# Second feed-forward block: seven products from chunk 2 on, its first plain down inside the first pair, and another order in the mixer

## The chip, the cores and the metric

The kernel runs on one core of a Trainium2 chip. Its engines work side by side, each through its own list of instructions: PE (TensorE, matmuls into eight PSUM banks of 128 x 512 fp32), DVE (VectorE), ACT (ScalarE), POOL (GpSimd) and SP (SyncE, which here only issues loads). Instructions of different engines wait for each other by semaphores. The metric is the time of one execution on the device in microseconds (us), the median of several runs.

## The reference

One layer on x of 512 tokens by 1024, all in fp32: half a SwiGLU feed-forward block, a token mixer, half a second feed-forward block, each with an RMS norm before and after.

```python
def swiglu(x, w_gu, w_down):                     # w_gu 1024 x 5632, w_down 2816 x 1024
    gate, up = jnp.split(x @ w_gu, 2, axis=-1)
    return (jax.nn.silu(gate) * up) @ w_down

def hybrid_mixer(h, ...):
    proj = h @ w_in                              # x_lru 512, gate_lru 512, q 512, k 128, v 128
    ...
    y_lru = rg_lru(x_lru, ...) * jax.nn.gelu(gate_lru)     # convolution of width 4, gates, a linear scan over tokens
    y_attn = sliding_window_sink_attention(q, k, v, sinks) # window 128, blocks of 128 queries, 8 heads of 64
    y = jnp.concatenate([rms_norm(y_lru, g_lru_out), rms_norm(y_attn, g_attn_out)], axis=-1)
    return y @ w_o

def reference(x, ...):
    x = x + 0.5 * rms_norm(swiglu(rms_norm(x, ffn1_pre_g), ffn1_w_gu, ffn1_w_down), ffn1_post_g)
    x = x + rms_norm(hybrid_mixer(rms_norm(x, mix_pre_g), ...), mix_post_g)
    x = x + 0.5 * rms_norm(swiglu(rms_norm(x, ffn2_pre_g), ffn2_w_gu, ffn2_w_down), ffn2_post_g)
    return x
```

## The kernel before

**Numbers.** Each fp32 operand is split into two parts of the faster matmul format: a high part (a cast by ACT) and a low part (operand less high part, by DVE). A product is three matmuls: high x high, high x low, low x high. Names carry it: `whi`/`wlo` are the parts of a weight, `xh`/`xl` of the input, `hh`/`hl` of the hidden activations. Activations are kept turned: the width lies on the partitions, the 512 tokens along the row.

**Stages.** Block 1 (letter a), mixer (letters mx, q, gt, wo), block 2 (letter b). The 2816 hidden columns are 22 chunks of 128. In a block the first chunks are *plain* (`Hidden.classic`): gate and up of each chunk are 24 matmuls over 512 columns each. The rest comes in pairs of chunks (`Hidden.quad`): gate and up of two chunks are a 2 x 2 block product, which is made with seven half-size products instead of eight (Winograd's form). Each of the seven is 24 matmuls of 256 columns into one of three banks A, D, B; their weight operands are sums of blocks of the weight (units p, q, r, s, t, u, v of `add_quad`), their input operands are parts and sums of the input: b11, b21, b22 are parts of xh and xl themselves, t1 to t4 come from `Turned.sums` (four DVE sums of 128x256 and two ACT casts per slice k of four) and `Turned.lows` (the DVE low parts). The down product is plain for the first group (`first_down`: for each half dh of the width, four token blocks, a bank each, which ACT copies to a `stage` and POOL sends to memory), and of the seven-product kind for groups of four chunks (`seven_down`: 84 matmuls of 512 columns, partial results added in memory by POOL's transfers). In block 2 `CLASSIC2` = 6 chunks are plain, `GROUPS2` starts (0, 6), (6, 10), and three groups have a seven down.

**Weights.** `W` holds one list of raw loads and one list of units in the order in which PE takes them. `load` issues the next raw on SP's queue into one of five buffers of 1 MB (`NRAW`); a buffer comes free when its last unit is split. `round` (or `cast`) does ACT's cast of the next unit, `fill` DVE's low part. `take(ahead)` hands PE the next unit and first fills `ahead` units beyond it; `later(n, fn)` runs fn at the n-th take from now. In `add_quad` a sum of weight blocks is made in place in the raw buffer by DVE (`combine`), ahead of the cast that reads it. The rows of x for the residual (`x_rows`) occupy two of the five raw buffers from late in block 1 to the end of the mixer.

**Order.** It is written out by hand: each engine runs its instructions in the order in which the program issues them. The mixer interleaves, by hand, PE's gate products (`gt`, `pump`), scores, softmax (`exps`, `normalise`), transposes of the probabilities (`turn_p`, ACT copies `pa`, POOL's masked copies `pc`), values (`po`), the LRU (`decay_b`: DVE's `th`; `root`; `scan`) and gelu (`gelu_b`: DVE, then a tanh on ACT; `gelu_c`, `gelu_d`), and at the end the product with w_o (`wo`), whose weights are `whi_wo60`, `wlo_wo60` and so on.

**The mixer's end.** `boundary` makes the four token blocks' rows (`Rows.steps`: norm, residual, norm), transposes them (`turn`, `turned`) and runs the gate/up of chunks 0 and 1 of block 2 meanwhile, in halves of the tokens (`one`, then `k_high` and `k_low`, the products named `mn`). Then the rows are stored to `x_hbm` for the last residual, `classic` runs chunks 2 to 5 with the sums of k = 0, 1 between them, `Turned.blocks` makes the b11 copies (eight ACT casts), and `first_down` runs with the sums of k = 2, 3.

Of the kernel before, what the change touches and what calls it, by code (L numbers as in the profile page):

```python
# [8 lines left out]
F32 = mybir.dt.float32  # L9
# [24 lines left out]
CLASSIC1, CLASSIC2 = 4, 6  # L34
SEVEN_DOWN1, SEVEN_DOWN2 = (4, 16), (6, 18)
# [12 lines left out]
class Weights:  # L48
# [60 lines left out]
    def take(self, ahead=AHEAD):  # L109
        self.fill(1 + ahead, ahead >= AHEAD)  # L110
# [11 lines left out]
def tile_layer(ctx: ExitStack, tc: tile.TileContext, out: bass.AP, **ins: bass.AP):  # L122
# [72 lines left out]
    def add_quad(w_gu, f, name):  # L195
# [11 lines left out]
        def unit(block, n, pre=None):  # L207
            def cast(raw):
                assert ry < W.loaded
# [4 lines left out]
            def low(raw, hi, lo):  # L214
                dve.tensor_sub(lo, of(block), hi.bitcast(F32))

            W.unit(block[0], cast, low, pre)
# [58 lines left out]
    def add_layer(w_gu, wd, name, groups, classic, seven, done):  # L276

        for f0, f1 in groups:
            for f in range(max(f0, done), f1, 2):
                (add_gate_up if f < classic else add_quad)(w_gu, f, name)  # L280
# [250 lines left out]
    class Turned:  # L531


        def __init__(self, name, pre, forms=False):
            self.name, self.pre, self.t = name, pre, {}
# [16 lines left out]
        def sums(self, k):  # L552
# [12 lines left out]
            self.made = n, highs, (t13, t24)  # L565

        def lows(self, k):

            n, highs, xs = self.made
            for s, h, x, names in zip(("t13", "t24"), highs, xs, (("t1", "t3"), ("t2", "t4"))):  # L570
                lo = t2k(f"{s}l_{n}", F32R)
                dve.tensor_sub(lo, x, h.bitcast(F32))
                for i, m in enumerate(names):
                    self.t[m, k] = h[:, HALF[i]], lo[:, HALF[i]]

        def blocks(self):

            l, r = HALF
            for k in range(4):
                b11 = t2k(f"b11_{self.name}{k}", F32R)  # L580
                for x, sl in zip(self.xs[k], HALF):
                    act.copy(b11[:, sl], x.bitcast(F32)[:, l])
                self.t["b11", k] = b11[:, l], b11[:, r]
                for m, sl in (("b21", l), ("b22", r)):
                    self.t[m, k] = tuple(x[:, sl] for x in self.xs[k + 4])

    class Rows:


        def __init__(self, name, x, gain, scale, eps, nxt):  # L590
            self.name, self.x, self.scale, self.eps, self.nxt = name, x, scale, eps, nxt
# [32 lines left out]
        def steps(self, tb):  # L624
# [3 lines left out]
            for dh in range(2):  # L628
                x = self.x[tb][:, HALF_D[dh]]
                dve.scalar_tensor_tensor(x, self.z.pop((tb, dh)), self.rs, x, op0=ALU.mult, op1=ALU.add)  # L630
                self.sum_square(tb, dh, x, "x")
            yield
# [21 lines left out]
    def boundary(rows, produce, parts, turns, fills, ahead, name):  # L654
# [68 lines left out]
        W.fill(2)  # L723
        k_high(ws, banks, xs, r, range(KD))
# [1014 lines left out]
```

## Time and profile before

| | us |
|---|---|
| runs (3) | 858.18, 858.59, 859.12; median 858.59 |
| profiled execution | 858.53, span 856.3, granted clock 0.998 |
| PE busy | 845.0 (99%), 5534 matmuls |
| DVE busy | 656.8 (77%) |
| ACT busy | 529.2 (62%) |
| POOL busy | 153.6 (18%) |

A row of the timeline gives start, duration, engine, line, operation, output <- inputs, shapes, how many follow each other, and in square brackets how long the engine sat idle before it and what ended that. Starts on PE are the more exact ends of a stage: a matmul's own duration overlaps the next one. On the chain of waits a row is start, length and what ran. "A, x3" means three such instructions in a row. The span of the profile is 2.2 us shorter than the execution's time.

### The profile page before, as it was taken

The page shows a single profiled execution, that of the slowest core. Times are in us where ns is not written, and L with a number is a line of the kernel's source. Part 1 is how long each engine was busy: PE and PEld are TensorE (multiplying, and loading weights), DVE is VectorE, ACT ScalarE, POOL GpSimd, SP SyncE. Part 2 cuts the span into 40 slices and gives each one's busy share as a digit, 9 for nine tenths or more (in the row PEclk, how much of TensorE's full clock was granted, in tenths as well). Part 3 has the DMA queues.
Part 4 walks back from the last instruction along what each step waited for, and adds up shares of the span by engine and source line. Part 5 has one row for each costly group of instructions (what it writes and reads, how often), then busy time and mean ns, then how long its engine had stood idle before and what let it go on. Part 6 is the DMA issues. An engine that isn't in the chain of part 4 may idle for free. (4 is left out here: it accounts for less than half of the span.)

```text
span 856.3 us, 14126 instructions
## 1 busy us (share of the span) xinstructions
PE 845.0 (99%) x5534; PEld 768.4 (90%) x5534; DVE 656.8 (77%) x897; ACT 529.2 (62%) x901; POOL 153.6 (18%) x185
## 2 busy tenths in 40 slices
PE   9999999999999999999999999999999999999996
PEld 8888999989989998998777889888998998998995
DVE  4989898887988867777888675357488789888856
ACT  6647567566566555658765776246466657657542
POOL 2022005014025021016103030001101303204402
PEclk9999999999999999999999999999999999999999
DMA  8265339739559454113141508244433946938912
GB/s 247 100 197 197 122 102 236 188 98 236 153 108 263 159 189 131 50 50 99 41 107 27 193 29 295 74 145 152 148 99 103 236 130 150 219 99 199 275 68 98
DMA packets 92902, 124.41 MB, mean 145 GB/s; under 512 B 5865, under 2 KB 62501, under 8 KB 92837
## 3 DMA queue, kind: packets, MB, share of 16 engines
q1 hardware_dynamic: 76276, 86.68, 32.4%
q0 software_dynamic: 16416, 36.71, 19.2%
q8 instruction: 43, 0.70, 0.3%
q14 instruction: 23, 0.18, 0.1%
q10 hardware_dynamic: 144, 0.13, 0.0%
HBM read 93.10 MB, written 30.41 MB: 144 GB/s over the span
## 5 line engine op out<-in xcount | busy, mean ns | idle before, releaser
L925 POOL DMA_DIRECT2D yp_b<-stage x42 | 36.4, 1133 | 149.1 <-ACT stage L922 140.4
L925 POOL DMA_DIRECT2D yp_a<-stage x42 | 37.0, 1131 | 146.2 <-ACT stage L922 140.7
L1173 POOL DMA_DIRECT2D yp_b<-stage x8 | 4.3, 541 | 91.7 <-ACT stage L1172 90.9
L1144 PE MATMUL yal<-whi_ad,hha 128*128 128x512 f32 x48 | 18.9, 393 | 0.0
L1146 PE MATMUL yal<-whi_ad,hla 128*128 128x512 f32 x48 | 18.7, 390 | 0.0
L1145 PE MATMUL yal<-wlo_ad,hha 128*128 128x512 f32 x48 | 18.7, 389 | 0.0
L1144 PE MATMUL yb<-whi_bd,hhb 128*128 128x512 f32 x48 | 18.7, 389 | 0.0
L1145 PE MATMUL yb<-wlo_bd,hhb 128*128 128x512 f32 x48 | 18.7, 389 | 0.0
L1146 PE MATMUL yb<-whi_bd,hlb 128*128 128x512 f32 x48 | 18.7, 389 | 0.0
L177 DVE TENSOR_TENSOR wlo_bd<-raw_bd,whi_bd 128x1024 fp32r<-128x1024 f32 x10 | 12.2, 1223 | 8.1 <-ACT whi_bd L172 8.1
L177 DVE TENSOR_TENSOR wlo_wo<-raw_wo,whi_wo 128x1024 fp32r<-128x1024 f32 x8 | 10.3, 1308 | 7.2 <-ACT whi_wo L172 7.2
L177 DVE TENSOR_TENSOR wlo_ad<-raw_ad,whi_ad 128x1024 fp32r<-128x1024 f32 x10 | 12.2, 1222 | 3.9 <-ACT whi_ad L172 3.9
L1289 POOL TENSOR_TENSOR xcl<-xc,xch 128x512 fp32r<-128x512 f32 x4 | 5.1, 1296 | 52.3 <-ACT xch L1288 52.3
L1377 POOL TENSOR_SCALAR_AFFINE_SELECT pc<-pa 128x384 f32<-128x384 f32 x8 | 5.4, 674 | 46.4 <-ACT pa L1376 46.3
L600 ACT ACTIVATE sqxr<-x_rows 128x512 f32<-128x512 f32 x16 | 10.0, 631 | 5.6 <-DVE x_rows L630 5.6
L407 PE MATMUL gt<-xh_mx,whi_gt 128*128 128x512 f32 x32 | 13.2, 412 | 0.0
L1145 PE MATMUL ybl<-wlo_bd,hhb 128*128 128x512 f32 (+1 forms) x36 | 13.2, 366 | 0.0
L1144 PE MATMUL ybl<-whi_bd,hhb 128*128 128x512 f32 (+1 forms) x36 | 13.2, 366 | 0.0
L1146 PE MATMUL ybl<-whi_bd,hlb 128*128 128x512 f32 (+1 forms) x36 | 13.2, 365 | 0.0
L407 PE MATMUL pq<-xh_mx,whi_q 128*128 128x512 f32 x32 | 13.0, 408 | 0.0
L1691 ACT ACTIVATE ysq<-yp_b 128x512 f32<-128x512 f32 (+1 forms) x9 | 5.2, 582 | 12.4 <-DVE yp_b L1690 11.7
L550 POOL TENSOR_TENSOR xg_f<-xh_f,xl_f 128x256 f32<-128x256 f32 x8 | 5.8, 760 | 39.5 <-DVE xl_f L481 39.5
(1831 smaller groups left out, 3698.0 us busy)
## 6 DMA issues: line engine op xcount, KB each, us to landing
yp_a<-stage POOLq DMA_DIRECT2D x50, 256.0 KB, 7.0
yp_b<-stage POOLq DMA_DIRECT2D x50, 256.0 KB, 7.9
raw_ad<-in_ffn_w_down SPq DMA_DIRECT2D x4, 1024.0 KB
raw_bd<-in_ffn_w_down SPq DMA_DIRECT2D x4, 1024.0 KB
xn<-in_x SPq DMA_DIRECT2D x8, 256.0 KB, 3.8
x_rows<-in_x POOLq DMA_DIRECT2D x4, 512.0 KB, 11.1
yp_a<-yp_a POOLq DMA_DIRECT2D x8, 256.0 KB, 10.6
raw_q<-in_w_in SPq DMA_DIRECT2D x4, 512.0 KB, 4.2
```

What stands on the lines that cost most here:

```text
L177: low.tensor_sub(two(lo, x), x, two(hi.bitcast(F32), x))
L407: pe.matmul(ps, hi[:, k, :], xh, start=start, stop=False)
L550: pool.tensor_add(o, *(x.bitcast(F32)[:, HALF[h]] for x in self.xs[c]))
L600: act.activation(wt(f"sq{name}{self.name}{tb}{dh}"), src, AF.Square, accum_out=self.ss[name, tb][:, dh:dh + 1])
L925: pool.dma_start(o, st.rearrange("p (a b) -> p a b", a=2) if len(o.shape) == 3 else st, accum_op=ALU.add)
L1144: pe.matmul(ps, hh[:, blk], hi[:, k, cs], start=start, stop=False)
L1145: pe.matmul(ps, hh[:, blk], lo[:, k, cs], start=False, stop=False)
L1146: pe.matmul(ps, hl_[:, blk], hi[:, k, cs], start=False, stop=stop)
L1173: pool.dma_start(parts[tb, dh], st)
L1289: pool.tensor_sub(xl, xcs[ci], xh.bitcast(F32))
L1377: pool.affine_select(v4(pc)[:, 1:, :], v4(pa)[:, 1:, :], pattern=[[0, NB - 1], [1, P]], base=0, channel_multiplier=-1, compare_op=ALU.is_g ...
L1691: act.activation(wt(f"ysq{tb}{i}")[:, :c1 - c0], y, AF.Square, accum_out=ss[:, i:i + 1])
```

## The change

Block 2: only chunks 0 and 1 stay plain; chunks 2 to 5 become a group like the others, two quads and a seven down, so that four groups have seven downs. The plain down of chunks 0 and 1 (48 matmuls) is put inside the first quad, between its products A(b11) and D(t3) (`first_part`, handed down as `between` and `early`); during it one small unneeded matmul has written bank B. The sums and lows of k = 0, 1 are made at the end of `boundary` (`beside`, `Turned.forms`), those of k = 2, 3 in `first_part`. The first group reads b11 from xh and xl; the eight b11 copies for later groups are now transfers on POOL's queue, at the eighth take after the plain down. The stores to `x_hbm` move into `Rows.steps`, one per token block, with a weight load behind the second and the fourth; the two loads at the first group's fourth take go.

Both blocks: the sums of weight blocks in `add_quad` are issued on DVE behind the cast of the unit before, ahead of or behind that unit's low part, and no longer by the unit that is cast next.

Mixer: `decay_b` of groups 2 and 3 behind `q_parts(1)`; `root` of 2 and 3 behind `products(1)`; `gelu_b`, `gelu_c` of group 1 behind `scan(3)`; `gelu_b`, `gelu_c` of group 2 and `gelu_d` of 1 behind the casts that follow.

DVE in the mixer, around the low part of the second pair of heads' query (qT1l); th0 to th3 are the LRU's decay terms, vd a difference of v. Before:

```order
L1366 TENSOR_TENSOR sc01_4574<-sc01_4574,den01_4572 128x512
L1299 SCALAR_TENSOR_TENSOR th2_4489<-m2_4558,th2_4489 128x512
L1299 SCALAR_TENSOR_TENSOR th3_4504<-m3_4561,th3_4504 128x512
L1314 TENSOR_TENSOR qT1l_4629<-pq1_4583,qT1h_4628 128x512
L1510 TENSOR_TENSOR vd_4618<-v_4617 128x384
L177 TENSOR_TENSOR wlo_gt4_0_4686<-raw_gt4__4416,whi_gt4_0_4685 128x1024
```

After:

```order
L1405 TENSOR_TENSOR sc01_4574<-sc01_4574,den01_4572 128x512
L1353 TENSOR_TENSOR qT1l_4627<-pq1_4583,qT1h_4626 128x512
L1338 SCALAR_TENSOR_TENSOR th2_4489<-m2_4558,th2_4489 128x512
L1338 SCALAR_TENSOR_TENSOR th3_4504<-m3_4561,th3_4504 128x512
L1550 TENSOR_TENSOR vd_4618<-v_4617 128x384
L177 TENSOR_TENSOR wlo_gt4_0_4686<-raw_gt4__4416,whi_gt4_0_4685 128x1024
```

qT1l has moved ahead of th2 and th3.

ACT in the mixer, from the first cast of the last attention half's output weight (whi_wo40) on; pa30 and pa31 are copies of the last transposed probabilities, gq is the gelu's polynomial (ACTIVATE gq<-gq its tanh). Before:

```order
L172 CAST whi_wo40_5112<-raw_wo40_4852 128x1024
L1427 ACTIVATE gq1_5038<-gq1_5038 128x512
L1419 COPY gt2_5130<-gt2_5040 128x512
L1421 ACTIVATE gq2_5132<-gt2_5130 128x512
L1376 COPY pa30_5149<-pt30_5144 128x512
L1376 COPY pa31_5161<-pt31_5156 128x512
L172 CAST whi_wo41_5166<-raw_wo41_5024 128x1024
L1419 COPY gt3_5182<-gt3_5134 128x512
L1421 ACTIVATE gq3_5184<-gt3_5182 128x512
L172 CAST whi_wo60_5186<-raw_wo40_4852 128x1024
L1427 ACTIVATE gq2_5132<-gq2_5132 128x512
L478 ACTIVATE yah3_5206<-po3_5193,cols_136 128x512
```

After:

```order
L172 CAST whi_wo40_5112<-raw_wo40_4852 128x1024
L1458 COPY gt2_5128<-gt2_5040 128x512
L1460 ACTIVATE gq2_5130<-gt2_5128 128x512
L1415 COPY pa30_5147<-pt30_5142 128x512
L1415 COPY pa31_5159<-pt31_5154 128x512
L172 CAST whi_wo41_5164<-raw_wo41_5024 128x1024
L1458 COPY gt3_5180<-gt3_5132 128x512
L1460 ACTIVATE gq3_5182<-gt3_5180 128x512
L172 CAST whi_wo60_5184<-raw_wo40_4852 128x1024
L1466 ACTIVATE gq1_5038<-gq1_5038 128x512
L493 ACTIVATE yah3_5203<-po3_5190,cols_136 128x512
L453 ACTIVATE sq_a3_5206<-po3_5190 128x512
```

The tanh of gq1 stood ahead of gt2 and of both pa copies; it now stands behind whi_wo60, and that of gq2 goes further down.

ACT at the start of block 2, behind the last turned rows (xg). Before, the weights of chunks 2 and 3 (bg2, bu2) and the silus of chunks 0 and 1:

```order
L172 CAST whi_bg2_0_5859<-raw_bg2__5760 128x1024
L172 CAST whi_bu2_0_5863<-raw_bu2__5763 128x1024
L172 CAST whi_bg2_1_5976<-raw_bg2__5760 128x1024
L172 CAST whi_bu2_1_5982<-raw_bu2__5763 128x1024
L739 ACT_TABLE_LOAD
L739 ACTIVATE gsb0_6013<-mn0_5692 128x512
L739 ACTIVATE gsb1_6017<-mn2_5777 128x512
L755 CAST hhb0_6021<-usb0_6015 128x512
L755 CAST hhb1_6025<-usb1_6019 128x512
L739 ACTIVATE gsb2_6029<-pgb2_5988 128x512
```

After, from the bank copy of the first quad (bb2) on, behind the casts whi_bp2, whi_bd00, those of the sums of k = 0, 1 and the same silus; t13h and t24h are the casts of the sums, `stage` the copies of the plain down's banks:

```order
L867 COPY bb2_6032<-ab2_6030 128x512
L172 CAST whi_bd01_6064<-raw_bd01_5774 128x1024
L579 CAST t13h_f22_6089<-ta_f22_6087 128x512
L579 CAST t24h_f22_6090<-tb_f22_6088 128x512
L1209 ACTIVATE stage_6109<-yb000_6071 128x512
L1209 ACTIVATE stage_6112<-yb001_6072 128x512
L1209 ACTIVATE stage_6115<-yb002_6073 128x512
L1209 ACTIVATE stage_6118<-yb003_6074 128x512
L213 CAST whi_bq2__6121<-raw_bx2__5545 128x1024
L579 CAST t13h_f23_6126<-ta_f23_6124 128x512
L579 CAST t24h_f23_6127<-tb_f23_6125 128x512
L213 CAST whi_br2__6156<-raw_bx2__5545 128x1024
```

Where ACT cast plain gate/up weights it now casts down weights, sums, stages and the quad's units q and r in turn.

The diff, cut to its core:

```diff
-CLASSIC1, CLASSIC2 = 4, 6
-SEVEN_DOWN1, SEVEN_DOWN2 = (4, 16), (6, 18)
+CLASSIC1 = 4
+SEVEN_DOWN1, SEVEN_DOWN2 = (4, 16), (2, 18)
...
-        unit(a, "p")
-        unit(c, "q", combine(dve.tensor_sub, c, a, c))
-        unit(c, "r", combine(dve.tensor_sub, c, d, c))
-        unit(b, "s", combine(dve.tensor_add, a, c, a))
-        unit(a, "t", combine(dve.tensor_sub, b, b, c))
+        unit(a, "p", mid=combine(dve.tensor_sub, c, a, c))
+        if early:
+            early()
+        unit(c, "q", "p", post=combine(dve.tensor_sub, c, d, c))
+        unit(c, "r", "q", mid=combine(dve.tensor_add, a, c, a))
+        unit(b, "s")
+        unit(a, "t", "r", mid=combine(dve.tensor_sub, b, b, c))
         unit(d, "u")
-        unit(b, "v")
+        unit(b, "v", "t")
...
-    GROUPS2 = [(0, 6), (6, 10), (10, 14), (14, 18), (18, 22)]
-    add_layer(w2, ins["ffn2_w_down"], "b", GROUPS2, CLASSIC2, SEVEN_DOWN2, 0)
+    GROUPS2 = [(0, 2), (2, 6), (6, 10), (10, 14), (14, 18), (18, 22)]
+    add_layer(w2, ins["ffn2_w_down"], "b", GROUPS2, 2, SEVEN_DOWN2, 0)
...
+        def forms(self):
+            l, r = HALF
+            for k in range(4):
+                self.t["b11", k] = tuple(x[:, l] for x in self.xs[k])
+                for m, sl in (("b21", l), ("b22", r)):
+                    self.t[m, k] = tuple(x[:, sl] for x in self.xs[k + 4])
+            for fn in (self.sums, self.lows):
+                for k in range(2):
+                    fn(k)
         def blocks(self):
             l, r = HALF
             for k in range(4):
                 b11 = t2k(f"b11_{self.name}{k}", F32R)
                 for x, sl in zip(self.xs[k], HALF):
-                    act.copy(b11[:, sl], x.bitcast(F32)[:, l])
+                    pool.dma_start(b11[:, sl], x[:, l])
...
+            if self.store:
+                self.store(tb)
...
         W.fill(2)
+        if beside:
+            beside()
         k_high(ws, banks, xs, r, range(KD))
...
-            seven(A, "b11", True)
+            soon = 2 if early else AHEAD
+            seven(A, "b11", True, 1 if early else begin)
+            if early:
+                pe.matmul(B, self.nxt.xs[0][0][:, :P], self.nxt.xs[0][0], start=True, stop=True)
             act.copy(B, A)
-            seven(D, "t3", True)
+            if early:
+                early()
+            seven(D, "t3", True, soon)
...
     normalise(0, 1)
-    for ci in (2, 3):
-        decay_b(ci)
     preload(AF.Sqrt)
     root(0)
     root(1)
     q_parts(1, pq)
+    turn_p(0, 0)
+    for ci in (2, 3):
+        decay_b(ci)
     dve.tensor_sub(vd[:, P:], v[:, P:], v[:, :T - P])
-    turn_p(0, 0)
-    root(2)
-    root(3)
     pump(1)
     turn_p(0, 1)
     products(1)
+    root(2)
+    root(3)
     W.cast(1)
...
-             2: [(scan, 2), (gelu_d, 0), (gelu_b, 1), (gelu_c, 1)]}
+             2: [(scan, 2), (gelu_d, 0)]}
...
     scan(3)
-    gelu_b(2)
-    gelu_c(2)
-    gelu_d(1)
+    gelu_b(1)
+    gelu_c(1)
     pump(100)
     values(3)
...
     W.cast(4)
+    gelu_b(2)
+    gelu_c(2)
+    gelu_d(1)
     gelu_b(3)
...
+    def store(tb):
+        pool.dma_start(x_hbm[tb * P:(tb + 1) * P], x_rows[tb])
+        if tb % 2:
+            W.load()
...
-    hs = hid.classic(CLASSIC2, banks, {3.5: [(n2.sums, 0)], 4: [(n2.lows, 0)], 4.5: [(n2.sums, 1)], 5: [(n2.lows, 1)]}, AHEAD - 1)
-    n2.blocks()
-    first_down(hid, hs, CLASSIC2, parts2, {(0, 0): (n2.sums, 2), (0, 2): (n2.lows, 2), (1, 2): (n2.sums, 3), (1, 4): (n2.lows, 3)})
-    middle_downs(hid, GROUPS2[1:-1], parts2)
+    hs = hid.classic(2, banks, {})
+
+    def first_part():
+        W.fill(2)
+        steps = {(0, 0): [(n2.sums, 2)], (0, 1): [(W.cast, 2), (n2.sums, 3)],
+                 (1, 0): [(n2.lows, 2), (W.fill, 1), (W.cast, 2), (n2.lows, 3), (W.fill, 2)]}
+        first_down(hid, hs, 2, parts2, steps, 0)
+        W.later(8, n2.blocks)
+
+    middle_downs(hid, GROUPS2[1:-1], parts2, first_part)
```

More of the change, by code (lines that the diff above doesn't have):

```diff
@@ L107, in later, with take @@
         self.todo.append((self.taken + n, fn, args))
-    def take(self, ahead=AHEAD):
-        self.fill(1 + ahead, ahead >= AHEAD)
+    def take(self, ahead=AHEAD, early=True):
+        self.fill(1 + ahead, early and ahead >= AHEAD)
         self.taken += 1
@@ L205, in of, with unit @@
             return W.tiles[block[0]][:, :, block[1]]
-        def unit(block, n, pre=None):
+        split = ""
+        def unit(block, n, after="", mid=None, post=None):
             def cast(raw):
-                assert ry < W.loaded
+                assert ry < W.loaded and after in split
                 hi, lo = w_tiles(4, 2 * P, f"{name}{n}{f}_")
@@ L652, in turned, with boundary @@
                 fn(c, h, self.tp[h, c - c % 2][:, HALF[c % 2]])
-    def boundary(rows, produce, parts, turns, fills, ahead, name):
+    def boundary(rows, produce, parts, turns, fills, ahead, name, beside=None):
         nxt = rows.nxt
@@ L802, in seven_right, with quad @@
             self.steps = [lambda: self.low("s2"), last_sum, lambda: self.low("s4"), lambda: self.low("a22")]
-        def quad(self, f, last, ahead, seven_down=False):
+        def quad(self, f, last, ahead, seven_down=False, early=None, begin=AHEAD):
             n = f"{self.name}{f}"
@@ L810, in seven @@
             def seven(b, form, first, ahead=AHEAD):
-                hi, lo = W.take(ahead)
+                hi, lo = W.take(ahead, not early)
                 for j in range(2):
@@ L849, in quad @@
             W.later(1, low_parts, u2, 0)
-            seven(A, "b22", False, ahead)
+            seven(A, "b22", False, 3 if early else ahead)
             act.activation(g1, A, AF.Silu)
@@ L869, in beside @@
                     fn(k)
+            if n == 2:
+                for i in range(2):
+                    self.gate(i, banks[2 * i])
+                    self.up(i, banks[2 * i + 1])
+                for i in range(2):
+                    self.split(i)
             for f in range(2, n):
```

75 lines of the change are left out of this document (41 added, 34 removed).

## Prediction, made before the changed kernel was run

> **What bounds the kernel now.** I read the page's busy times first, then TensorE's (PE's) waits, then the stretches of the second block, then the chain that ended last.
>
> ```profile
> PE 845.0 (99%) x5534; PEld 768.4 (90%) x5534; DVE 656.8 (77%) x897; ACT 529.2 (62%) x901; POOL 153.6 (18%) x185
> ```
> ```profile
> PE sc L1338 <- DVE qT1l L1314: 0.7, 1, 0.7
> ```
>
> PE is busy for 845.0 of 856.3 us, and its longest wait after the start is 0.7. So time is gained only by giving PE fewer columns, or from the few small holes, and lost only where another engine or a load makes PE wait. Next, three stretches of the second block. The columns are the stretch, its length, the busy time of PE, of the weight load (PEld), DVE, ACT and POOL with instructions in brackets, the granted clock, the DMA share and GB/s.
>
> ```profile
> 532.50:608.50 76.00, 76.00 (x337) 62.92 (x336) 41.78 (x56) 33.24 (x51) 2.91 (x6) 1.00 0.36 118
> 608.70:649.00 40.30, 40.30 (x338) 40.30 (x337) 30.23 (x31) 22.34 (x29) 1.22 (x3) 1.00 0.35 119
> 649.10:668.10 19.00, 19.00 (x86) 15.72 (x85) 16.88 (x20) 14.35 (x23) 6.78 (x8) 1.00 0.71 167
> ```
>
> The first is the plain gate/up of chunks 2 to 5 and the plain down of chunks 0 to 5, the second two quads (one group's gate/up by seven products), the third a seven down. PE is busy in all of each, at clock 1.00, while DVE is busy in 55% of the plain stretch, 75% of the quads and 89% of the seven down: the stages that the change adds are those in which the other engines have least room. The starts of the same stages on the chain of waits give the prices:
>
> ```profile
> 532.55 0.23 PE pgb L407
> ...
> 608.73 2.87 PE ab L817 x24
> ...
> 649.05 0.23 PE yab L1154
> ...
> 668.11 2.87 PE ab L817 x24
> ```
>
> From 532.55 to 608.73 stand 192 plain gate/up matmuls (4 chunks, gate and up, 8 slices of the width, 3 partial products) and 144 plain down matmuls: 76.18 us for 336, 0.2267 each. From 608.73 to 649.05 stand 2 x 7 x 24 = 336 half-wide (256 column) matmuls: 40.32 us, 0.120 each. From 649.05 to 668.11 stand 84 full-wide ones of a seven down: 19.06 us, 0.2269 each.
>
> **The change, part by part.** *Block 2, PE's own work.* The 76.18 us are replaced by two quads (40.32), one seven down (19.06), the plain down of chunks 0 and 1 alone (2 halves x 2 chunks x 4 token blocks x 3 = 48 matmuls, 48 x 0.2267 = 10.88) and one dummy full-wide matmul (0.23): 70.49. That is -5.69 us, none of it beside other work since PE has no room elsewhere.
>
> By the Trainium skill, page "TensorE: Matmul & The Clock Gate", section "Wait — 56ns, not 53.3ns?", a warm matmul starts N / 2.4 GHz plus some 2.5 ns after the one before, which would make an estimate of 215.8 ns for 512 columns and 109.2 for 256. By it this term would be 336 x 0.2158 = 72.5 against 36.7 + 18.1 + 10.4 + 0.2 = 65.4, so -7.1 in place of -5.69. The rows above say 226.7 and 120.0; the measurement decides.
>
> *Mixer order.* Three of PE's holes are touched:
>
> ```profile
> 410.29 0.33 PE L1338 MATMUL sc<-kTh,qT1l 64*128 64x128 f32 x2 [0.72 <-DVE qT1l L1314]
> ...
> 455.78 0.39 PE L409 MATMUL gt<-xh_mx,wlo_gt 128*128 128x512 f32 x1
> 456.58 0.92 PE L1391 MATMUL po<-pa,v 128*64 128x256 f32 x3 [0.41 <-ACT pa L1376]
> ...
> 467.20 0.39 PE L1617 MATMUL wo<-whi_wo,yah 128*128 128x512 f32 x1
> 467.70 0.50 PE L1617 MATMUL wo<-wlo_wo,yah 128*128 128x512 f32 x1
> ```
> ```profile
> 408.35 1.28 DVE L1299 SCALAR_TENSOR_TENSOR th<-m,th 128x512 f32<-128x512 f32 x2
> 409.56 0.68 DVE L1314 TENSOR_TENSOR qT1l<-pq,qT1h 128x512 fp32r<-128x512 f32 x1
> ...
> 457.99 1.93 DVE L177 TENSOR_TENSOR wlo_wo<-raw_wo,whi_wo 128x1024 fp32r<-128x1024 f32 x1 [2.60 <-ACT whi_wo L172]
> ```
> ```profile
> 454.28 0.63 ACT L1427 ACTIVATE gq<-gq 128x512 f32<-128x512 f32 x1 [2.86 <-DVE gq L1424]
> ...
> 455.96 1.05 ACT L1376 COPY pa<-pt 128x512 f32<-128x512 f32 x2
> ```
>
> At 410.29 the scores of the second pair of heads wait 0.72 for qT1l, which stands on DVE behind two decay products (th2, th3, 1.28 together). They now stand behind it, and qT1l can start as soon as its ACT half is there: -0.7, a few hundredths left. Late in exchange are th2 and th3, by 0.68; the roots on ACT that read them are moved too, behind the copies pa of the first pair and the products of the next, and only the LRU's scans read those.
>
> At 456.58 PE waits for pa31: 0.57 between the start of the matmul at 455.78 (0.23 long) and that of the next, and 0.2 more a moment later for the masked copy pc. On ACT the two copies pa30, pa31 (455.96, 1.05) stand behind the tanh of gq1 (454.28), which waited 2.86 for DVE. That tanh now stands eight instructions later, behind whi_wo60. The copies are then held only by PE's own transposes, which end near 453.4, so they are done near 454.1, two microseconds early: -0.77. Behind them the cast whi_wo41 and so DVE's wlo_wo41 (457.99, waited 2.60 for that cast) move up by about 2 us, then scan 3, gq1, its tanh and the split of the last attention rows, at whose end stands wlo_wo60. PE waits 0.27 for it (467.70 less 467.20 less 0.23); this goes too: -0.27. The gelu of channel group 1 is late in exchange, but it feeds only the LRU norm, whose matmuls stand at the end of this stage. Mixer: -1.74. From below the gain is 0 (the holes reappear behind the moved tanh, which now waits just ahead of yah3); from above -1.76, all three holes whole.
>
> *The first pair in block 2.* Here PE gets half-wide products, and must not wait while ACT and DVE make down weights, the width-4 sums of the input (`forms`, `sums`, `lows`) and the first quad's weights all at once. DVE's rows and ACT's price it:
>
> ```profile
> 583.19 0.42 DVE L559 TENSOR_TENSOR ta_f<-xg_f 128x256 f32<-128x256 f32 x1
> ...
> 584.73 1.22 DVE L177 TENSOR_TENSOR wlo_bd<-raw_bd,whi_bd 128x1024 fp32r<-128x1024 f32 x1
> 585.87 0.69 DVE L572 TENSOR_TENSOR t13l_f<-ta_f,t13h_f 128x512 fp32r<-128x512 f32 x1
> ```
> ```profile
> 524.22 1.16 ACT L172 CAST whi_bg<-raw_bg__5760 128x1024 fp32r<-128x1024 f32 x1
> ...
> 538.54 1.04 ACT L172 CAST whi_bg<-raw_bg__5980 128x1024 fp32r<-128x1024 f32 x1
> ...
> 590.47 2.64 ACT L1172 ACTIVATE stage<-yb 128x512 f32<-128x512 f32 x4
> ```
>
> In order of time: ACT is free of the turned rows at 524.22 (there stood the first weight cast of before), casts whi_bp2 by 525.15 and whi_bd00 a microsecond later, and DVE follows with their lows by 527.7; PE asks for the first at 532.4 and the second at 535.5. The tight place is later. Count from the end of the dummy matmul. PE then does 48 x 0.227 = 10.90, D(t3) 2.88, and reads the low part of the third weight, wlo_br2, in the third matmul of A(t2): at 14.0. The other chain: bank copy bb2 0.7 (it waits for the dummy), cast whi_bd01 1.05, wlo_bd01 1.22, four sums at 0.385 (four start between 583.19 and 584.73) 1.54, their cast 0.62, four stages 2.1 (four in 2.64 with the overlap), whi_bq2 0.95, wlo_bq2 1.25, the weight sum 1.14, two lows 1.2, the second weight sum 1.14, wlo_br2 1.22: 14.1, or 14.3 with handovers. So PE waits 0.1 to 0.3; I take +0.3. Bounds: 0, if ACT is ahead of the stages, and +2.2 (rival A). After it DVE has one unit per 2.88 us of PE and gains 1 us with each.
>
> *Edits at no cost.* The weight sums behind the copy come one DVE instruction (1.22) later, in both blocks; a unit is made four products, 4 x 2.88 us, ahead, and DVE has 10 us spare in a quad stage; without that cover it is up to 1.2 per product that waits. The b11 copies leave ACT (8 casts) for POOL's queue after the eighth take; the first group reads the input's own parts instead, and the copies are first read in the next group, a quad and a seven down (20.2 + 19.1) after their issue. The mixer's output goes to HBM by block inside the row steps; x_rows hold two of the five weight buffers, and blocks 1 and 3 are each followed by a weight load. Three of the stores are issued where POOL has no other work; the last one carries a load that is needed soon:
>
> ```profile
> 458.80 2.27 POOL L1576 TENSOR_TENSOR xc<-xc,gt 128x512 f32<-128x512 f32 x1
> ...
> 513.66 0.53 POOL L1658 DMA_DIRECT2D x_hbm<-x_rows  x1 [0.84 <-DVE x_rows L630]
> ```
> ```profile
> x_hbm<-x_rows POOLq DMA_DIRECT2D x1, 512.0 KB, 6.0
> ```
> ```profile
> raw_wo<-in_w_o SPq DMA_DIRECT2D x4, 512.0 KB, 5.4
> ...
> raw_ax__3202<-in_ffn_w_gu SPq DMA_DIRECT2D x2, 512.0 KB, 18.5
> ```
>
> It is issued behind the same row step as before (513.66) and lands 6.0 later, 519.7. The load of the first down weights, raw_bd00, takes that buffer, and raw_bd01, raw_bx4 and raw_by4 stand behind it in SP's queue, wanted 10 us and more after it. By the nearest load of 512 KB (raw_wo, 5.4) it lands at 525.1, when ACT asks for it. Behind it ACT has four casts of the sums, a table load, two silus and two casts before PE's first down product at 535.5; by the same count that leaves 1.2 us, so PE waits only if it lands after 526.3.
>
> The sum is against the profiled execution, 858.53 (span 856.3 and 2.2 around it; 0.06 under the median of 858.59, which I add): 858.53 - 5.69 - 1.74 + 0.3 = 851.40, on the median's basis 851.4.
>
> **The rivals.** *A, the first pair starves.* Beside POOL's products (458.80, 2.27) one wlo took 1.93 (457.99) and not 1.22, and the chain above has five such DVE instructions and no slack. POOL has only four short issues there, which speaks against it. Three slow ones make 3 x 0.71 = 2.1, so 853.5; all five 855.0.
> By the Trainium skill, page "SBUF — State Buffer", section "Who interferes with whom", DVE and GpSimd share one port pair under an exclusive lock, and a store issued from POOL's queue can starve for its descriptors while DVE holds it. The trace agrees in kind: 1.93 against 1.22.
>
> *B, the mixer's waits only move.* The tanh that now stands ahead of the last rows (yah3) may wait as long as the old one did (2.86), and qT1l for its ACT half; then the holes come back at yal and wo, and block 2's gain stands alone: 858.59 - 5.69 + 0.3 = 853.2. Against it: the copies that PE waits for stand ahead of that tanh.
>
> *C, the matmuls are the faster ones.* By the gap of the rule above the time would be 850.0; no row of this kernel has it.
>
> *D, slower than before: raw_bd00 is late.* From 526.3 on each microsecond costs one, and the kernel is slower than before once it lands after 526.3 + 7.2 = 533.5, a load of 13.8 us. One load of that kind in block 1 took 18.5 (the last row above), which gives 519.7 + 18.5 - 526.3 = 11.9 late and 863.3. Against it: the other 512 KB load above took 5.4, the store itself 6.0.
>
> **How the numbers follow.** Main 0.72, between 850.2 (no stall, all holes, and a microsecond of others) and 852.3 (a stall of 1.2); A 0.14; B 0.08; C 0.02; D 0.04, of which 0.025 ends slower. The prediction is the main's 851.4. The range 850.2 to 853.6 takes in the main, B, and the lower half of A: 0.72 + 0.08 + 0.07. About 1.7 us (0.2%) is what a measurement can tell from no change; main, A, B and C lie beyond it, so faster 0.96, same 0.015 and slower 0.025 (both D).
>
> **What would show it.** Chunks 2 to 5 as fourteen rows of 24 half-wide matmuls, 2.88 us each, and some 70.8 us from the first of them to the end of the first seven down;  sc with no wait over 0.2 for qT1l; no wait of po for pa; wo dense at wlo_wo60. A shows as a wait of PE at A(t2) or D(t3) for wlo_br2 or t13l over 0.5, with DVE rows near 1.9; B as waits at yal or wo; D as a wait of the first yb for whi_bd00. It is wrong if block 2's stage is longer than 72 us, or if a wait stands where none stood.

## The result and the profile after

The changed kernel takes 854.57 us (median of 5 runs, 853.61 to 854.76) against 858.84 for the kernel before on the same chip: ratio 0.9949, 95% interval 0.9935 to 0.9964. It is faster by 4.3 us, where 7.2 were forecast; the range ended at 853.6. The profiled execution took 854.44, with a span of 852.7. First the page's first part and PE's longest wait of the changed kernel:

```profile
PE 840.4 (99%) x5667; PEld 771.8 (91%) x5667; DVE 691.5 (81%) x929; ACT 549.3 (64%) x927; POOL 174.6 (20%) x207
```
```profile
PE wo L1665 <- DVE post_eps L1639: 2.4, 1, 2.4
```

A wait of 2.4 us stands where none stood: PE, at the product with w_o, for a value that DVE makes from the two norms of the mixer. It is longer than all three holes that the mixer's new order was to close. Next the second block: the stretch from the first quad to the end of the first new seven down (columns as in the prediction), and the starts on the chain.

```profile
534.60:605.40 70.80, 70.79 (x471) 65.16 (x470) 65.48 (x76) 49.91 (x73) 15.59 (x24) 1.00 0.56 163
```
```profile
534.64 2.88 PE ab L845 x24
...
548.66 2.87 PE db L845 x24
...
605.54 2.87 PE ab L845 x24
```

From 534.64 to 605.54 are 70.90 us, where the stage of before took 76.18: -5.28 against -5.4 in the forecast. The other engines are fuller, as feared (DVE 65.48 of 70.80, 92%), and still PE is busy in all of it. The one small wait in the first pair, PE's rows and then DVE's:

```profile
551.49 0.28 PE L845 MATMUL ab<-t24l_f,whi_br__6156 128*128 128x256 f32 x1
551.77 0.39 PE L845 MATMUL ab<-t24h_f,wlo_br__6157 128*128 128x256 f32 x1
```
```profile
550.50 1.22 DVE L220 TENSOR_TENSOR wlo_br__6157<-raw_bx__5545,whi_br__6156 128x1024 fp32r<-128x1024 f32 x1
```

The third matmul of A(t2) starts 0.28 behind the second, not 0.12: it waits for wlo_br2, done at 551.72. The dummy matmul ended at 537.76, so the chain counted in the prediction took 13.96 where 14.1 to 14.3 stood there, and PE waits 0.16.

The mixer's end is where the time went. PE's rows around the wait, then DVE's rows of the changed kernel, then the same work in the kernel before, with PE's row behind it:

```profile
477.72 0.62 PE L1665 MATMUL wo<-whi_wo,yal 128*128 128x512 f32 x2
480.75 0.50 PE L1665 MATMUL wo<-whi_wo,yah 128*128 128x512 f32 x1 [2.41 <-DVE post_eps L1639]
```
```profile
466.83 0.68 DVE L1469 SCALAR_TENSOR_TENSOR gq<-gq,gt 128x512 f32<-128x512 f32 x1
467.44 0.69 DVE L1463 SCALAR_TENSOR_TENSOR gq<-gq,gt 128x512 f32<-128x512 f32 x1
468.04 2.32 DVE L177 TENSOR_TENSOR wlo_wo<-raw_wo,whi_wo 128x1024 fp32r<-128x1024 f32 x1
470.28 2.38 DVE L1614 SCALAR_TENSOR_TENSOR xc<-gq,xc 128x512 f32<-128x512 f32 x2
...
478.26 2.36 DVE L177 TENSOR_TENSOR wlo_wo<-raw_wo,whi_wo 128x1024 fp32r<-128x1024 f32 x2
480.54 0.15 DVE L1639 TENSOR_SCALAR post_eps<-rms_mix 128x4 f32<-128x4 f32 x1
```
```profile
462.66 0.68 DVE L1430 SCALAR_TENSOR_TENSOR gq<-gq,gt 128x512 f32<-128x512 f32 x1
...
468.17 1.21 DVE L177 TENSOR_TENSOR wlo_wo<-raw_wo,whi_wo 128x1024 fp32r<-128x1024 f32 x1
469.30 1.28 DVE L1573 SCALAR_TENSOR_TENSOR xc<-gq,xc 128x512 f32<-128x512 f32 x2
...
476.19 2.36 DVE L177 TENSOR_TENSOR wlo_wo<-raw_wo,whi_wo 128x1024 fp32r<-128x1024 f32 x2
478.47 0.16 DVE L1598 TENSOR_SCALAR post_eps<-rms_mix 128x4 f32<-128x4 f32 x1
```
```profile
478.99 0.40 PE L1617 MATMUL wo<-whi_wo,yah 128*128 128x512 f32 x1
```

`balance` puts the sums for the two norms into a PSUM bank, rms_mix. The next wo bank of the fourth token block takes that bank over, so PE cannot go on until post_eps, its last reader, is done. In the kernel before post_eps ended at 478.63, and PE took the bank at 478.99 (the last row above): 0.36 to spare, with no wait to show for it. Now post_eps starts 2.07 later (480.54 against 478.47). Of this 0.70 is the later start of the whole profile (below), so 1.4 is the mixer's own. DVE comes to wlo_wo61 no later than before (468.04 against 468.17), and loses 2.2 in two rows: wlo_wo61 takes 2.32 and not 1.21, the products xc2, xc3 take 2.38 and not 1.28. On PE's side the three holes did close: after the two matmuls at 477.72 (0.227 each) it could go on at 478.17, which is 1.5 sooner than 478.99 when the 0.70 is taken off. So the wait, 2.5 between the starts of the matmuls, adds up: 1.5 that PE gained, less 0.36 to spare, and 1.4 by which the bank came late. Even with the bank at its old time, only 0.36 of PE's gain would have been kept. Beside DVE's two rows runs POOL, first after, then before:

```profile
467.60 1.68 POOL L1617 TENSOR_TENSOR xc<-xc,gq 128x512 f32<-128x512 f32 x1 [6.14 <-DVE gq L1469]
469.23 2.27 POOL L1617 TENSOR_TENSOR xc<-xc,gt 128x512 f32<-128x512 f32 x1
```
```profile
463.42 1.29 POOL L1576 TENSOR_TENSOR xc<-xc,gq 128x512 f32<-128x512 f32 x1 [2.35 <-DVE gq L1430]
464.67 1.29 POOL L1576 TENSOR_TENSOR xc<-xc,gt 128x512 f32<-128x512 f32 x1
```

Before, POOL made its products of channel groups 1 and 3 from 463.42 to 465.96, while DVE sat idle or did short work. They hang on the second product of gq1 (462.66 before, 466.83 after: it was put behind the first product of gq2), so they now fall on DVE's weight work, and both sides are slowed.

The profiled difference of 4.09 adds up from four places. The start of the program, ahead of any changed line, ran 0.70 later in this profile (the first product of block 1 at 36.91, before at 36.21); the mixer up to the first product of block 2 1.40 longer; block 2 up to its last matmul 5.29 shorter; what lies behind the last matmul, in the span and outside it, 0.90 shorter (9.69 before, 8.79 after).

### The profile page after: what moved, and what is told of

Same layout as the page of the kernel before. It is cut to its first block, busy times and chain, and to the rows that moved or that the text cites. A ratio compares the mean times of both kernels' runs of the same rounds, so it can differ in the third digit from the quotient of the medians.

```text
span 852.7 us, 14558 instructions
## 1 busy us (share of the span) xinstructions
PE 840.4 (99%) x5667; PEld 771.8 (91%) x5667; DVE 691.5 (81%) x929; ACT 549.3 (64%) x927; POOL 174.6 (20%) x207
## 5 line engine op out<-in xcount | busy, mean ns | idle before, releaser
L964 POOL DMA_DIRECT2D yp_b<-stage x56 | 49.3, 1143 | 187.3 <-ACT stage L961 168.7
L880 DVE TENSOR_TENSOR u2b<-u2b,db 128x512 f32<-128x512 f32 x10 | 6.9, 686 | 12.5 <-PE db L845 12.5
L880 DVE TENSOR_TENSOR u2a<-u2a,da 128x512 f32<-128x512 f32 x9 | 6.2, 687 | 12.5 <-PE da L845 12.5
L1665 PE MATMUL wo<-whi_wo,yah 128*128 128x512 f32 x32 | 12.8, 399 | 2.4 <-DVE post_eps L1639 2.4
L873 ACT COPY u2b<-ab 128x512 f32<-128x512 f32 x10 | 5.9, 588 | 11.9 <-PE ab L845 11.9
L1748 POOL TENSOR_TENSOR yp_b<-yp_b,grow 128x512 f32<-128x512 f32 x6 | 7.8, 1293 | 27.1 <-ACT ysq L1741 27.0
L1665 PE MATMUL wo<-wlo_wo,ylh 128*128 128x512 f32 x32 | 12.6, 393 | 0.1
```

The costliest lines, as they stand in the source:

```text
L880: dve.tensor_add(u2, u2, D)
L964: pool.dma_start(o, st.rearrange("p (a b) -> p a b", a=2) if len(o.shape) == 3 else st, accum_op=ALU.add)
L1665: pe.matmul(wo_banks[tb][dh], x, w[:, k, :], start=start and k == 0 and w is hi and not xp, stop=stop and k == 1 and xp == 1, skip_group_c ...
```

## The experiments

All are timed against the kernel before on their own chip in 5 rounds. "New block 2" stands for all of the change but the mixer's order.

| run | what it is | us | ratio to before, 95% interval |
|---|---|---|---|
| e1 | new block 2, old mixer | 852.35 | 0.9926 (0.9914 to 0.9939) |
| e2 | before, new mixer | 860.64 | 1.0025 (1.0015 to 1.0035) |
| e3 | changed, gelu_d of 1 early | 852.16 | 0.9925 (0.9912 to 0.9937) |
| e4 | changed, low parts behind post_eps | 852.98 | 0.9932 (0.9918 to 0.9945) |
| e5 | changed, three moves | 850.52 | 0.9907 (0.9894 to 0.9921) |
| e6 | changed, POOL's order | 852.70 | 0.9935 (0.9921 to 0.9948) |
| e7 | before, weight sums behind the cast | 858.39 | 1.0001 (0.9992 to 1.0009) |
| e8 | e1, b11 copies by ACT | 853.16 | 0.9938 (0.9926 to 0.9951) |
| e9 | e1, stores together | 852.59 | 0.9930 (0.9916 to 0.9944) |
| e10 | changed, again | 854.33 | 0.9957 (0.9943 to 0.9971) |
| e11 | e1, first mixer edit alone | 853.70 | 0.9948 (0.9935 to 0.9961) |
| e12 | e1, second mixer edit alone | 852.69 | 0.9934 (0.9922 to 0.9947) |
| e13 | before, 22 more transfers | 857.96 | 0.9996 (0.9987 to 1.0005) |
| e14 | e5 with the old order around qT1l | 850.49 | 0.9910 (0.9897 to 0.9924) |

**The two halves apart: e1 and e2.** The mixer's part of the change has four places: `turn_p(0, 0)`, `decay_b` of 2 and 3 and their `root`s around qT1l; the step table entry 2; the gelu calls behind `scan(3)`; those behind `W.cast(4)`. e1 takes these lines in the old text (its diff to the changed kernel is the diff of the change, reversed, at these places); e2 puts the new text of them into the kernel before.

> The changed kernel with the mixer's order of before; block 2 and the weight sums stay changed. Theory M (the loss is the mixer's new wait of 2.4 us at the bank of rms_mix, the rest of the change does what was forecast): block 2 alone, -5.3 us, so about 853.5 against 858.8, and no wait of PE for post_eps. Rival B2 (block 2 or the earlier stores also lose what is missing): the wait goes, yet the time is 854.5 or more.

> The kernel before with the mixer's new order alone. Theory M: the three holes close (-0.6, -0.75, -0.3) and a wait of 2.4 us at wo for post_eps opens, so +0.8 to +1.2: 859.6 to 860.0, slower by about 0.1%. Rival B2: the mixer gains its 1.7 as forecast, 857.1, and the wait comes only together with block 2.

The halves add up: 6.2 gained by e1, 2.1 lost by e2, 4.1 together, where the whole change measured 4.3 (4.0 when timed again, e10). The mixer's order made the kernel slower by itself, which neither the forecast nor one of its rivals had. e2 shows the same 2.4 for post_eps without the new block 2, so the rival is out:

```profile
PE wo L1619 <- DVE post_eps L1600: 2.4, 1, 2.4
```

Both sizes were off: e2 lost 0.9 more than the theory allowed, and e1 gained 0.9 more, of which more below. In e2's profile (861.6, the longest of its eight runs) a part of the loss is another one: behind the wait, from 482.20 to 483.91, the matmuls of the wo product start 0.43 apart and not 0.23, and the granted clock is 0.57 from 481.0 to 484.3. From the matmul that waited to the first product of block 2 it takes 30.14 there and 28.98 in e10's profile, so some 1.2 of that run's loss lies here. Whether the other runs of e2 have such a stretch too is not shown.

**What makes the wait: e3, e4, e6.** Three single moves in the changed kernel:

```diff
# e3
     rows_high(3)
+    gelu_d(1)
     rows_low(3)
...
     gelu_c(2)
-    gelu_d(1)
     gelu_b(3)
# e4
-    W.fill(2)
     balance()
+    W.fill(2)
# e6
-    for ci in (0, 2, 1, 3):
+    for ci in (0, 2, 3, 1):
         pool.tensor_mul(hl[ci], hl[ci], gts[ci] if ci in gts else gqs[ci])
```

> The changed kernel with one instruction moved: the second product of gq1 (gelu_d of group 1) stands on DVE ahead of the last attention rows (yal3), where DVE sat idle 1.83 us, and no longer behind the first product of gq2. Theory M with the cause in POOL's late products (they run beside DVE's wlo_wo61 and xc and each slows the other: 2.32 against 1.21, 2.38 against 1.28): POOL's two products start near 463.4 as in the kernel before, post_eps comes about 2.5 us earlier, the wait of 2.4 falls to 0.3 or less, 852.0 to 852.5. Rival, the lateness is that of the tanhs on ACT: post_eps moves by 0.6 (one DVE instruction) and the time is about 854.

> The changed kernel with the casts and low parts of the next two weights (wo00, wo01) issued behind the balance of the two norms and not ahead of it. Theory M (what PE waits for is only that post_eps frees the bank of rms_mix, and ahead of post_eps stand two low parts, 2.36 us, that are needed later): post_eps at about 478.3, the wait is 0 to 0.2, 852.2; the rescales may start up to 0.7 later, so up to 852.9. Rival (PE waits for the LRU's rows or the rescales, not the bank): the wait moves to the first LRU product and the time stays 854 or more.

> The changed kernel with POOL's product of group 3 ahead of that of group 1, nothing else. Group 3's operands are there by 460.3, POOL is idle from 461.5 to 467.6. Theory of contention (of the 2.1 us by which post_eps is late, 1.1 are wlo_wo61 at 2.32 instead of 1.21 beside POOL, and 1.1 the products xc2, xc3 that wait for POOL's second product): one POOL product less runs beside DVE and DVE no longer waits for it, post_eps 1.1 earlier, the wait 2.4 becomes about 1.3, 853.4. Rival (the lateness is the tanhs' order on ACT and DVE, POOL does not matter): 854.5, unchanged.

e3 is 2.1 to 2.4 us faster than the changed kernel with one DVE instruction moved; e4 1.3 to 1.6 faster with the same LRU, but post_eps ahead of two weight parts (PE then waits 0.8 for a low part, wlo_wo, instead). So it is the bank, and POOL's late products are what makes it late. e6 confirms the second on its own: PE's wait falls to 1.5, and 852.70 is better than the 853.4 that the theory of contention gave.

```profile
PE wo L1665 <- DVE post_eps L1639: 1.5, 1, 1.5
```

e3's rows show where POOL beside DVE went to, DVE's first, then POOL's:

```profile
461.79 0.69 DVE L1469 SCALAR_TENSOR_TENSOR gq<-gq,gt 128x512 f32<-128x512 f32 x1 [0.70 <-ACT gq L1466]
...
464.34 2.31 DVE L177 TENSOR_TENSOR wlo_wo<-raw_wo,whi_wo 128x1024 fp32r<-128x1024 f32 x1
```
```profile
463.82 1.73 POOL L1617 TENSOR_TENSOR xc<-xc,gt 128x512 f32<-128x512 f32 x1
```

Here wlo_wo60 is the part that runs beside POOL (2.31), and PE waits 0.6 for it instead. In e4 the same meeting falls out the other way round, POOL's row and then DVE's:

```profile
466.63 3.41 POOL L1617 TENSOR_TENSOR xc<-xc,gq 128x512 f32<-128x512 f32 x1 [6.15 <-DVE gq L1469]
```
```profile
467.07 1.22 DVE L177 TENSOR_TENSOR wlo_wo<-raw_wo,whi_wo 128x1024 fp32r<-128x1024 f32 x1
...
471.33 0.69 DVE L1614 SCALAR_TENSOR_TENSOR xc<-gq,xc 128x512 f32<-128x512 f32 x1 [2.44 <-POOL xc L1617]
```

DVE's part keeps its 1.22, POOL's product takes 3.41 and not 1.29, and DVE then waits 2.44 for POOL. One of the two pays, or both, and the order of their starts does not tell which: POOL's row starts ahead of DVE's in the changed kernel (467.60 and 468.04) as in e4 (466.63 and 467.07). The changed kernel itself, run again, falls out as e4 did (e10 below).

**Each mixer edit alone: e11 and e12.** e11 is e1 with the first place of the mixer's diff (th2, th3, roots behind qT1l), e12 with the other three (gelu):

```diff
# e11, against e1
-    for ci in (2, 3):
-        decay_b(ci)
...
+    turn_p(0, 0)
+    for ci in (2, 3):
+        decay_b(ci)
...
-    turn_p(0, 0)
-    root(2)
-    root(3)
...
+    root(2)
+    root(3)
# e12, against e1
-             2: [(scan, 2), (gelu_d, 0), (gelu_b, 1), (gelu_c, 1)]}
+             2: [(scan, 2), (gelu_d, 0)]}
...
+    gelu_b(1)
+    gelu_c(1)
-    gelu_b(2)
-    gelu_c(2)
-    gelu_d(1)
...
+    gelu_b(2)
+    gelu_c(2)
+    gelu_d(1)
```

> The kernel of e1 with the first mixer edit alone: th2, th3 and their roots behind qT1l; the gelu stays as before. PE's wait of 0.72 there closes. Theory G (what PE gains ahead of the two norms' balance is worth only the slack of the bank of rms_mix, some 0.3, since post_eps stands at the end of DVE's own chain): 0.2 to 0.4 under e1, 852.0, and a wait of 0.3 for post_eps appears. Rival (the holes simply add up, as in the prediction): 0.65 under e1, 851.7, no wait.

> The changed kernel with the old order around qT1l and the new order of the gelu: the counterpart of e11. In e11 the softmax and the LRU ran 1.2 us later on DVE and ACT from th2, th3 on (1.91 beside POOL, and the roots ahead of the next table load), and PE met it at pa with 1.8. Theory S (two parts make the wait of 2.4: 1.2 from the late th2, th3, the rest from the late second product of gq1 and POOL beside DVE): the hole of 0.72 is open again, pa has no wait, and the wait for post_eps falls to 0.6 to 1.2; 853.3 to 853.9. Rival (the gelu's order makes all of the wait): 2.4 as before plus the hole, 855.0.

e11 refutes both of its theories: the hole at qT1l closes (0.64 between starts), and yet it is 1.35 slower than e1. PE's longest wait in e11, then in e12, then DVE's row of th2 and th3 in e11:

```profile
PE po L1430 <- ACT pa L1415: 1.8, 1, 1.8
```
```profile
PE wo L1665 <- DVE post_eps L1639: 1.5, 1, 1.5
```
```profile
409.49 1.91 DVE L1338 SCALAR_TENSOR_TENSOR th<-m,th 128x512 f32<-128x512 f32 x2
```

th2 and th3, now beside POOL's masked copies, take 1.91 for the pair and not 1.28, their roots on ACT wait for them, and behind the roots stand a weight cast, a table load (at 413.02, in e1 at 411.62) and the next softmax. So the whole softmax side runs later, and with the gelu in its old place PE meets that at pa with 1.8 where 0.4 stood. e12 has the wait for post_eps at 1.5 and not 2.4, and is faster than both edits together by 1.6 (852.69 against 854.33). In size it lies below the 853.3 that theory S gave at best, so the split of the wait into two parts holds only roughly: some 0.9 from the first edit, 1.5 from the second. In time the first edit is the dearer one. Against the kernel before on its own chip e1 gains 6.2, e12 5.6, e11 4.7 and the whole change again (e10) 4.0, so the gelu's order alone costs 0.7, the order around qT1l alone 1.6, and both 2.2.

**Edits that were to cost nothing: e7, e8, e9.** e7 puts the seven new `unit` lines of `add_quad`, as the diff of the change has them, into the kernel before; e8 and e9 change e1:

```diff
# e8
-                    pool.dma_start(b11[:, sl], x[:, l])
+                    act.copy(b11[:, sl], x.bitcast(F32)[:, l])
# e9
-        pool.dma_start(x_hbm[tb * P:(tb + 1) * P], x_rows[tb])
-        if tb % 2:
-            W.load()
+        if tb == NB - 1:
+            for t in range(NB):
+                pool.dma_start(x_hbm[t * P:(t + 1) * P], x_rows[t])
+            W.load(2)
```

> The kernel before with the sums of weight blocks behind the cast in both blocks, nothing else. Forecast: hidden, 858.6 within 0.3. Rival (they give the 0.9 us that block 2 gained beyond its forecast, of which 0.4 lies behind the last computation and 0.5 outside the span): 857.7.

> The kernel of e1 (changed block 2, the mixer's order of before) with the eight b11 copies made by ACT as before, at the same place, and not by POOL's transfers. Forecast: hidden either way, 852.4 within 0.3. Rival 1 (ACT was short of room in the first group): PE waits for a weight cast, 853 or more. Rival 2 (the eight transfers of POOL's queue are what shortens the end of the program): the last computation ends as in e1 but the time is 0.5 to 0.9 longer.

> The kernel of e1 (new block 2, the mixer's order of before) with all four stores to x_hbm, and the two loads that follow them, issued behind the last token block, as before, and not block by block. Forecast: raw_by2 comes some 12 us later but still 10 us before its use, raw_bd00 a little later since three more stores share the way; 852.4 within 0.3. Rival D of the prediction (raw_bd00 late): PE waits at the first down product, 853 to 857. Rival (the stores' order is what ends the program 0.9 us sooner): the last computation ends as in e1, the time is 0.9 longer.

The sums cost nothing and bring nothing (858.39 against 858.34). The stores' place is worth 0.2 (0.4 against each one's own kernel before), less than the intervals tell apart; PE does not wait for the first down weights in either kernel, so rival D of the prediction is out. The b11 copies are another matter: left on ACT they would cost 0.8 (1.0 against each one's own kernel before),

```profile
PE ybb L1193 <- ACT ybb L958: 0.7, 1, 0.7
```

since ACT's copy of a down bank in the new first group then comes 0.7 late. The rival in its expectation was right in kind, with another victim.

**The changed kernel again, and the program's end: e10, e13.** e10 has no edit. e13 adds transfers to the kernel before, into a spare place in HBM that nothing reads, behind the first down of block 2:

```diff
+    spare = hbm.tile([22 * P, T], F32, name="spare")
+    for i in range(22):
+        pool.dma_start(spare[i * P:(i + 1) * P], n2.xs[i % KD][0].bitcast(F32))
```

> The changed kernel as it is, once more, on the chip of these runs. In its first profile the head, before any changed line, ran 0.9 us later than in the kernels of e1 to e8 (36.91 against 35.9 to 36.2 at the first product of block 1). If that belongs to the moment and not to the kernel, about 853.6; if it belongs to the kernel, 854.5 again.

> The kernel before with 22 more transfers on POOL's queue (128 x 512 each, into a spare piece of memory, behind the first down of block 2), as many as the changed block 2 has more; they compute nothing. The kernels with the new block 2 end 0.9 us sooner behind their last computation (0.4 in the span, 0.5 outside it). Theory T (the number of transfers on that queue does it): the last computation ends as before, the time is 0.9 less, 857.5. Otherwise 858.4 or a little more.

e10's profile has its head at the usual place (35.98), so the 0.70 of the first profile is of the moment. It goes with the granted clock: from 10 to 12 us this was 0.50 to 0.56 in the three profiles with a late head (the changed kernel, e9, e14: 36.66 to 37.01), and 1.00 in all others (35.75 to 36.21). In size the expectation failed: 853.6 were expected for that case, and 854.33 came. The four runs of e10 that were not profiled have mean granted clocks of 0.993 to 0.996, the profiled one (853.94) has 0.999; where the clock fell in the four is not on record. PE's wait in e10 is again 2.4, but here POOL pays, its row first and then DVE's:

```profile
466.70 3.41 POOL L1617 TENSOR_TENSOR xc<-xc,gq 128x512 f32<-128x512 f32 x1 [6.15 <-DVE gq L1469]
```
```profile
467.13 1.22 DVE L177 TENSOR_TENSOR wlo_wo<-raw_wo,whi_wo 128x1024 fp32r<-128x1024 f32 x1
...
471.40 0.69 DVE L1614 SCALAR_TENSOR_TENSOR xc<-gq,xc 128x512 f32<-128x512 f32 x1 [2.44 <-POOL xc L1617]
```

So one and the same kernel shows both outcomes, and post_eps comes late by either.

e13 leaves the 0.9 us behind the last matmul unexplained: its ratio cannot be told from 1. All profiles with the new block 2 have that gain, none without it has it; the order of the stores (e9), the b11 transfers (e8) and the sums (e7) do not make it. It stays open.

**A better version: e5 and e14.** e5 joins e3's and e6's moves, and puts only the casts of wo00, wo01 ahead of `balance`:

```diff
-    W.fill(2)
+    W.cast(2)
     balance()
+    W.fill(2)
```

> The changed kernel with three moves in the mixer: the second product of gq1 ahead of the last attention rows (as in e3), POOL's product of channel group 3 ahead of that of group 1 (it then runs while POOL is idle, before wlo_wo60, and not beside it), and the low parts of wo00, wo01 behind post_eps and the ratio (their casts stay ahead of them). Theory (the LRU's end, the bank of rms_mix and the rescales bound PE here, and POOL beside DVE costs both): wlo_wo60 takes 1.2 and PE's wait for it falls from 0.73 to 0; post_eps is read as soon as rms_mix is there, some 1.3 earlier than in e3, the rescales too; 851.0 to 851.4 against 852.2 for e3. Rival (the row chain behind the rescales ends at the same time whatever comes before): PE's waits move to tp_r and the time stays at 852.1.

> The kernel of e5 with the old order around qT1l. Theory S: e5 has no waits left behind the mixer, so the open hole costs its 0.65, but DVE and ACT run up to 1.2 sooner, which is worth nothing once PE is the bound: 851.1. Rival (even in e5 the row chain behind the mixer is bound by DVE and ACT, so that the earlier softmax is worth more than the hole): 850.5 or less.

e5 is 850.52, some 3.8 us faster than the changed kernel, and better than was expected of it. It gains 7.8 against the kernel before, where the forecast of the change was 7.2; the 0.9 behind the last matmul is in it. All of its waits of PE:

```profile
PE warm L1038 <- POOL ident masks.py:199: 1.4, 1, 1.4
PE a_first L442 <- ACT xh_a L493: 0.7, 1, 0.7
PE tp_r L674 <- DVE xn_r L666: 0.3, 1, 0.3
```

Only the last stands in the mixer, at its end (499.28), and the kernel before has it too (0.4). e14 is the same within what can be told (850.49), so the edit around qT1l is worth nothing even then: by the end of the attention products e5 stands 0.16 ahead of e14, not 0.64; the rest has gone in these products, which take 2.09 from the first to the wo product in e5 and 1.67 in e14.

## Why the prediction was wrong

*PE's own work in block 2: right.* -5.69 + 0.3 forecast, -5.28 measured for the stage, with 2.88 for each row of 24 half-wide matmuls. By the Trainium skill's gap (page "TensorE: Matmul & The Clock Gate", section "Wait — 56ns, not 53.3ns?") an estimate for the stage would be 65.4; the trace has 70.90. Rival C is out.

*The first pair: right.* The chain of twelve steps came out at 13.96 against 14.1 to 14.3. Rival A did not happen there: DVE's rows in the first pair are 1.22 to 1.23, and POOL has only issues of transfers there, 0.54 to 0.55 each.

*Mixer order: this step failed.* "The gelu of channel group 1 is late in exchange, but it feeds only the LRU norm, whose matmuls stand at the end of this stage" was taken as a cover and not priced. Behind that norm stood a PSUM bank that PE needs, with 0.36 to spare; the kernel before has the two rows (post_eps 478.47, the wo matmul at 478.99), but no wait stands there, and the bank is not in the sum. The holes themselves closed nearly as forecast (PE came to the bank 1.5 sooner in the first profile, 1.1 in e10's); that this would be kept was the error. The step was forecast at -1.74 and measured at +2.1 (e2), +2.0 (e10 less e1; 2.2 with each against its own kernel before, 1.7 between their profiled runs, both at a granted clock of 0.999). The same holds for th2, th3 and the roots: that "only the LRU's scans read those" was true and beside the point, since a softmax stands behind them in ACT's queue: this edit alone costs 1.6, the gelu's 0.7.

*Rival B* named the right part and stopped at zero: "block 2's gain stands alone". A wait that moves can also grow.

*Edits at no cost: right for the sums and stores* (e7, e9). For the b11 copies it held only as changed.

*What no step had:* 0.9 us behind the last matmul. It hid part of the error: without it the result would have been near 855.5.

## What to carry to other kernels

A hole closed ahead of a join is worth no more than the slack of the other side at that join, so look up when the join's last reader is done and when its bank or buffer is next needed, also where no wait is listed. Work that is moved to fill one engine's idle time leaves a place where its partner engine was idle too: ask which two engines now run side by side. A late instruction's cost is found behind it in its queue, not only among those that read its result.

## What the runs showed of the hardware that was not expected

DVE and POOL on SBUF operands slow each other almost by their full lengths: 2.32 against 1.21 (wlo_wo61), 2.38 against 1.28 (the pair xc), 3.41 against 1.29 (POOL's product in e4, while DVE kept its 1.22). The Trainium skill, page "SBUF — State Buffer", section "Who interferes with whom", states an exclusive lock on a port pair shared by the two, and these rows agree with it in kind. It also states that the order of issue decides who blocks; these rows can't settle that: POOL's row starts 0.43 to 0.44 ahead of wlo_wo61 in the first profile of the changed kernel, where both pay, and in e10, the same kernel, and e4, where wlo_wo61 keeps its 1.22. In all three DVE's product of gq, 0.69 long, is still running when POOL's row starts (it starts at 467.44, 466.53 and 466.47), and POOL's spans are rough, so its start may be its issue and not its first read. The prediction had cited the rule for the first pair of block 2, where POOL does not compute, and not for the mixer, where it does.
